# Ten plain-form steps for the sums, one PSUM exchange, and products placed by row work in a two-layer hybrid decoder

## The chip, the cores and the metric

The kernel runs on one core of a Trainium2 chip. The metric is the time of one execution in device microseconds (us). Most executions agree within 0.3%.

The engines named here are TensorE (PE, with its weight loads as PEld), VectorE (DVE), ScalarE (ACT), GpSimd (POOL) and SyncE (SP), whose queue issues most DMAs. SBUF is the memory that the engines compute from; PSUM holds what PE writes, in banks that are handed out as named buffers.

## The reference

One inference step of a two-layer decoder on a prompt of 1024 tokens and on 8 sequences of 4 new tokens (32 rows), width 1024. Each layer projects x, mixes along time in three groups of heads, projects back, and runs a gated ConvFFN of width 2816. Both residuals are scaled by ALPHA and normed.

```python
p_rw, p_gl, p_rt = split(x @ w_in[l])
y_a, sh, s_a = _rwkv7_mix(p_rw, ...)     # scan over time, state (H,64,64)
y_b, s_b = _gla_mix(p_gl, ...)           # chunks of 64
y_c, s_c = _ret_mix(p_rt, ...)           # chunks of 64
mix = concatenate([y_a, y_b, y_c], -1) @ w_out[l]
x = _layer_norm(ALPHA * x + mix, ...)
u = x @ w_up                             # 1024 -> 2 * 2816
c = conv_b + sum(conv_w[j] * buf[:, j:j + t_] for j in range(3))
a, b = split(c, 2)
f = (gelu(a) * b) @ w_down               # 2816 -> 1024
x = _layer_norm(ALPHA * x + f, ...)
```

Outputs are y of all tokens and the new states of every mixer and of the convolution.

## The kernel before

**Tiles and precision.** Channels lie on the 128 partitions and tokens along the free dimension, in three blocks n = 0, 1, 2 of 384, 384 and 288 columns (`NB`); block 2 holds the 32 sample tokens and the last 256 prompt tokens. Every large product is made of three matmuls (`mm3`, L140 in the trace): operands are split into a high and a low part (`split`, L197: ACT makes the high part, POOL or DVE the low one), and high x high, low x high and high x low are summed in PSUM. Small products of the mixers use plain 32-bit operands.

**Order of the tensor engine.** `Tensor` keeps its own clock `t`, to which each matmul adds its columns times passes over 2400 (`order`), and chains every PE instruction to the one before it, so PE's order is the order of emission. The mixers are written as generators (`Stream`), which yield either a delay from the table `AFTER` or an event. `run` goes round: of all streams that are ready on that clock it steps the first in the list. The streams of the recurrent chains stand first and those of the large projections last (`filler`), so a projection's product (three matmuls of a `gemm` step) is emitted when no chain step is ready. DVE, ACT and POOL are ordered by the framework's own scheduler, by program order and a simulated timeline.

**Stages of a layer.** First the projection for the first token block (`group_a(0)`, tile `pa`). Then the RWKV mixer: streams `chains`, `grams`, `toks`, `fronts` (tiles `gps`, `xps`, `tps`, `ups`, `zy`, `sp`, `up`), with `groups()` as filler (the rest of `pa`, then `group_b`, tile `gt`). Then GLA and retention (tiles `gsp`, `gop`, `gup`, `rsp`, `rop`, `ytp`), with the rest of `gt` and the output projection (`out_projs`, tile `po`) at the end of the list. Then the ConvFFN.

**ConvFFN.** There are 22 pairs of up tiles, j = 0 to 21 (tile j and tile j + 22). The plain form (`up_plain`, tile `pu`) multiplies each of the two tiles by all three blocks: eight half products of 12 matmuls for the two prompt blocks, four for the sample block. The other form (`up`) takes the two tiles and two prompt blocks as a 2 x 2 block product with seven products in place of eight (tiles `pa`, `pg`, `pb`, `pc`, `pf`, `pd`, `pe`), and the sample block as before (tile `p`). It needs sums of the weights, formed on DVE for each tile, and sums of x1 (`qs`), formed once by the generator `sums()`. That generator is stepped from `then(j, i, n)` at the places named in `times`, with i the half of the pair and n the block. Before the change, j = 0 to 3 are plain and `sums()` has five steps: four for k = 0 to 3 of its first loop, and one for its whole second loop, which writes over the first four tiles of x1's block 1. Its temporaries come from the ring of six buffers "u" that the up projections use too.

The down products of the pair j - 2, j - 1 (tile `pd`, `downs`) are emitted in the middle of tile j (`between`). Each of 24 has six matmuls and is read by DVE into `acc`; in the first group (L1664) the read also adds the residual x1, high and low part in two instructions, later (L1660) it is one add.

**PSUM.** Two pools matter: "g" (`pg`) with three buffers and "d" (`pd`) with five. Each tag hands out its buffers in turn, and a product waits until the one that held its buffer before has been read. `bank(n, name)` takes "g" for block 2 and "d" for the others. In `up`, the second product (`pg`, read at L1596) is in "g" and the third (`pb`, read at L1610) in "d"; the down products after it are in "d".

Of the kernel before, what the change touches and what calls it, by code (L numbers as in the profile page):

```python
# [18 lines left out]
P = 128  # L19
# [17 lines left out]
FB, BB = 2, 3  # L37
GB = 2
# [64 lines left out]
class Tensor:  # L103


    def __init__(self, tc, engine):
        self.tc, self.engine, self.t, self.last, self.posts, self.held = tc, engine, 0.0, None, [], None
        Event.clock = self.clock
# [4 lines left out]
    def order(self, ins, cols, passes):  # L113
        if self.held is not None:
            self.held.append((ins, cols, passes))
            return
        ins = ins.ins
        if self.last is not None:
            self.tc.add_manual_dep(ins, self.last.name, mybir.DependencyInfo(mybir.DependencyClass.NoSync, mybir.DependencyReason.DATA),
                                   reason="order of the tensor engine")  # L120
        self.last = ins
        self.t += max(0.025, cols * passes / 2400)

# [14 lines left out]
    def matmul(self, out, lhsT, rhs, start, stop):  # L138
        cols = int(np.prod(rhs.shape[1:]))
        self.order(self.engine.matmul(out, lhsT, rhs, start=start, stop=stop), cols, 4 if rhs.dtype == F32 else 1)  # L140

    def transpose(self, out, in_, identity):
        self.order(self.engine.transpose(out, in_, identity), identity.shape[1], 4)
# [10 lines left out]
    def run(self, streams, filler):  # L154

        streams = list(streams)
        while streams:
            self.flush(self.t)
            ready = [s for s in streams + filler if s.at() is not None and s.ready <= self.t + 0.02]
            if not ready:  # L160
                t = [s.ready for s in streams + filler if s.at() is not None] + [p[0] for p in self.posts]
                self.t = max(self.t, min(t)) + 0.001
                continue
            s = ready[0]
            if not s.step(self.clock):
                (streams if s in streams else filler).remove(s)
# [3 lines left out]
def step_kernel(ctx: ExitStack, tc: tile.TileContext, xT, wA, wB, wO, wU, wD, pp, pb, lora, bg, bgk, shT, cvT, srw, sgl, srt,  # L170
# [150 lines left out]
    for l in range(depth):  # L321
# [1052 lines left out]
        run([Stream(g) for g in (loads(0), loads(1), gla_backs(), fronts(0), ret_backs(), fronts(1), yrows(), ln1_steps())] + filler + [Stream(out_projs())], [])  # L1374
# [98 lines left out]
        def sums():  # L1473
# [30 lines left out]
            for k in range(4):  # L1504
                d = apart(G, x(1, k + 4), x(1, k))
                two(t3[0][:, k], t3[1][:, k], d, G)
                d = apart(V, x(1, k), x(0, k))
                minus(V, x(1, k + 4), d)
                two(t2[0][:, k], t2[1][:, k], d, G)
                f = new()  # L1510
                V.tensor_tensor(f, x(0, k + 4)[0], d, ALU.subtract)
                V.tensor_tensor(f, f, x(0, k + 4)[1], ALU.add)
                two(t4[0][:, k], t4[1][:, k], f, V)
                yield
# [3 lines left out]
            yield  # L1518
# [54 lines left out]
        def up(j, qs, late=False, between=lambda: None):  # L1573
# [18 lines left out]
            p2 = pg.tile([P, 512], F32, tag="g", name="pg")[:, :384]  # L1592
# [13 lines left out]
            pb_ = bank(0, "pb")  # L1606
# [47 lines left out]
        def down(m, n, group, hs, ws):  # L1654
# [4 lines left out]
            if group:  # L1659
                V.tensor_tensor(a, a, ps, ALU.add)  # L1660
            else:

                for x, y in zip(x1[n][:2], (ps, a)):
                    V.scalar_tensor_tensor(a, x[:, m].bitcast(F32), ALPHA, y, ALU.mult, ALU.add)  # L1664
# [11 lines left out]
        times = ((1, 0, 2), (1, 1, 2), (2, 0, 2), (2, 1, 2), (3, 1, 1))  # L1676
# [5 lines left out]
        for j in range(0, NJ - 2, 2):  # L1682
# [6 lines left out]
            elif j < 4:  # L1689
# [3 lines left out]
            hs = [a, up(j + 1, qs) if j >= 4 else up_plain(j + 1, lambda: None, then)]  # L1693
# [216 lines left out]
```

## Time and profile before

| | us |
|---|---|
| median of 3 runs | 3405.08 |
| lowest, highest | 3397.25, 3408.31 |
| profiled execution | 3395.68 |
| its span, first to last instruction | 3393.9 |

Mean granted PE clock of that execution: 0.945 of full speed. The sum to be made is against the profiled execution; it stands 9.4 us below the median of the runs shown.

The trace names an instruction by line, engine, operation and `out<-in` with the kernel's tile names. Nearly every matmul has the line of the helper (L140), so tiles tell them apart. "Idle" or a bracket gives how long the engine had nothing, and "<-" what ended it. A stage's row gives busy times of the engines and, behind them, the granted PE clock.

### The profile page before, as it was taken

How to read it: one execution, taken by the hardware profiler on the slowest of the kernel's cores; microseconds unless marked ns; L12 is line 12 of the kernel's file. 1: busy time of each engine (PE TensorE's matmuls, PEld its weight loads, DVE VectorE, ACT ScalarE, POOL GpSimd, SP SyncE). 2: the span in 40 equal slices, each digit the busy share in tenths (PEclk: the TensorE clock that was granted, in tenths of full speed). 3: DMA queues.
4: the chain of work that ended last, by engine and by line, in shares of the span. 5: the costliest groups of instructions: out<-in, count | busy, mean ns of one | idle time of the engine just before them, and what ended most of it. 6: DMA issues, size and time to landing. Idle time of an engine off the chain costs nothing. (4 is left out here: it accounts for less than half of the span.)

```text
span 3393.9 us, 59056 instructions
## 1 busy us (share of the span) xinstructions
PE 3103.4 (91%) x21618; PEld 2868.3 (85%) x21618; DVE 2374.4 (70%) x5085; ACT 1577.6 (46%) x3635; POOL 1575.1 (46%) x1512
## 2 busy tenths in 40 slices
PE   8889999998889999999788899998998899999995
PEld 8778887777889999999687787876778899999994
DVE  3586764566797777777857667644667977777778
ACT  6754432654534334434586534325545334344346
POOL 5542222144655555545675422221346555455556
PEclk9989999988999999999898899998989899999997
DMA  7443223443301111111264432233433011111111
GB/s 242 147 130 83 70 68 121 120 131 104 90 26 44 56 43 46 47 54 54 96 193 142 115 78 68 65 118 113 129 114 90 25 44 54 41 51 47 54 53 66
DMA packets 245566, 291.14 MB, mean 86 GB/s; under 512 B 76620, under 2 KB 158316, under 8 KB 245276
## 3 DMA queue, kind: packets, MB, share of 16 engines
q1 hardware_dynamic: 225004, 274.08, 26.8%
q10 hardware_dynamic: 20272, 13.29, 1.6%
q8 instruction: 170, 2.79, 0.3%
q14 instruction: 120, 0.98, 0.1%
HBM read 228.85 MB, written 58.43 MB: 85 GB/s over the span
## 5 line engine op out<-in xcount | busy, mean ns | idle before, releaser
L1433 DVE SCALAR_TENSOR_TENSOR c<-u,ppt,c 128x32 f32<-128x32 f32 (+3 forms) x704 | 514.2, 762 | 71.3 <-ACT c L1437 65.9
L197 POOL TENSOR_TENSOR wil<-wir,wih 128x512 fp32r<-128x512 f32 (+1 forms) x264 | 368.7, 1407 | 253.9 <-ACT wih L197 228.8
L140 PE MATMUL gt<-wih,xh 128*128 128x320 f32 (+1 forms) x1008 | 347.5, 346 | 4.6 <-DVE mx L404 4.6
L140 PE MATMUL gt<-wil,xh 128*128 128x320 f32 (+1 forms) x1008 | 322.2, 321 | 5.8 <-POOL wil L197 5.8
L1660 DVE TENSOR_TENSOR acc<-acc,pd 128x384 f32<-128x384 f32 (+1 forms) x480 | 239.4, 517 | 112.7 <-PE pd L140 110.2
L140 PE MATMUL gt<-wih,xl 128*128 128x320 f32 x896 | 286.0, 319 | 0.0
L197 ACT CAST wih<-wir 128x512 fp32r<-128x512 f32 (+1 forms) x296 | 184.5, 636 | 131.4 <-PE po L140 57.5
L140 PE MATMUL pa<-xh,wih 128*128 128x384 f32 (+1 forms) x576 | 208.7, 362 | 29.3 <-ACT wih L197 12.4
L653 DVE TENSOR_TENSOR tm<-U,N 96x60 f32<-96x60 f32 (+24 forms) x558 | 175.1, 314 | 81.2 <-DMA N<-gd 66.1
L140 PEld LDWEIGHTS gt<-wih,xh 128*128 128x128 f32 (+1 forms) x1008 | 192.1, 191 | 42.4 <-issue 24.6
L140 PE MATMUL pa<-xh,wil 128*128 128x384 f32 (+1 forms) x576 | 197.5, 343 | 12.5 <-POOL wil L197 12.5
L140 PEld LDWEIGHTS gt<-wil,xh 128*128 128x128 f32 (+1 forms) x1008 | 193.6, 192 | 10.1 <-POOL wil L197 8.6
L140 PE MATMUL pa<-xl,wih 128*128 128x384 f32 (+1 forms) x576 | 195.7, 340 | 0.8 <-POOL xl L197 0.8
L140 PEld LDWEIGHTS gt<-wih,xl 128*128 128x128 f32 x896 | 177.2, 198 | 0.0
L655 DVE TENSOR_TENSOR U<-U,tm 96x60 f32<-96x60 f32 (+24 forms) x558 | 164.6, 295 | 16.3 <-DMA tokd<-ev 0.3
L197 POOL TENSOR_TENSOR hl<-c,hh 128x384 fp32r<-128x384 f32 x132 | 139.4, 1066 | 53.0 <-ACT hh L197 53.0
L140 PEld LDWEIGHTS pa<-xh,wih 128*128 128x128 f32 x576 | 117.3, 204 | 44.0 <-ACT wih L197 13.6
L140 PE MATMUL po<-yh,wih 128*128 128x384 f32 (+1 forms) x384 | 136.1, 354 | 12.1 <-DVE ac L1349 10.2
L1437 ACT ACTIVATE c<-u,ppt 128x384 f32<-128x384 f32 x144 | 101.8, 708 | 85.3 <-DVE u L1633 39.9
L140 PEld LDWEIGHTS pa<-xh,wil 128*128 128x128 f32 x576 | 117.0, 203 | 16.6 <-POOL wil L197 16.6
L140 PE MATMUL po<-yl,wih 128*128 128x384 f32 (+1 forms) x384 | 128.1, 334 | 0.0
L140 PE MATMUL po<-yh,wil 128*128 128x384 f32 (+1 forms) x384 | 128.0, 333 | 0.0
(967 smaller groups left out, 10199.1 us busy)
## 6 DMA issues: line engine op xcount, KB each, us to landing
wir<-in_wA_dram SPq DMA_DIRECT2D x144, 256.0 KB
wir<-in_wO_dram SPq DMA_DIRECT2D x96, 256.0 KB
wir<-in_wB_dram SPq DMA_DIRECT2D x56, 320.0 KB
tokd<-ev SPq DMA_DIRECT2D x112, 160.0 KB
x<-rkvd SPq DMA_DIRECT2D x16, 576.0 KB
tk<-tokd SPq DMA_DIRECT2D x16, 480.0 KB
rkvd<-mx SPq DMA_DIRECT2D x36, 192.0 KB
tk<-tokd SPq DMA_DIRECT2D x16, 400.0 KB
```

The source lines that it names most:

```text
L140: self.order(self.engine.matmul(out, lhsT, rhs, start=start, stop=stop), cols, 4 if rhs.dtype == F32 else 1)
L197: return A.copy(dst_h, src), (le or G).tensor_tensor(dst_l, src, dst_h.bitcast(F32), ALU.subtract)
L653: V.tensor_tensor(tm, U[:, 0:nr, i:i + 1].to_broadcast([4 * ns, nr, 31 - i]), N[:, i:i + 1, i + 1:32].to_broadcast([4 * ns, nr, 31 - i]), ...
L655: V.tensor_tensor(U[:, 0:nr, i + 1:32], U[:, 0:nr, i + 1:32], tm, ALU.add)
L1433: V.scalar_tensor_tensor(cv[..., o:], uu[..., tap + o:tap + w], pc(PP_CV + 4 * t + tap), cv[..., o:], ALU.mult, ALU.add)
L1437: A.activation(c, src, AF.Identity, scale=pc(PP_CV + 4 * t + 2), bias=pc(PP_CV + 4 * t + 3))
L1660: V.tensor_tensor(a, a, ps, ALU.add)
```

## The change

- `Tensor` now also keeps the row work of each PE instruction: columns times passes (at most 2) times the share of the 128 rows. `thin()` is true if the row work of the last 3.4 us on the planner's clock is under 0.52 of what full rows would do.
- In `run`, if it is thin, the first ready stream that is a filler or in `dense` is stepped ahead of the first ready stream of the list. In the RWKV stage the filler is `groups()`; in the GLA and retention stage `dense` holds what is left of it and `out_projs`.
- `sums()` has ten steps: each k of the first loop in two (the first half is POOL and ACT work alone), the second loop in two. `times` has ten places, from j = 1 to the end of j = 5.
- The plain form is used for j = 0 to 5.
- In `up`, `pg` comes from "d" and `pb` from "g".
- The residual's high part is added in the first group of down products as before; its low part for block 1 in the same group, for block 0 in the second and for block 2 in the third.

```diff
...
 FB, BB = 2, 3
+
+DENSE, SPAN = 0.52, 3.4
 GB = 2
 BK, XB = 1, 2
 WBUFS, RAW = 4, 4
...
     def __init__(self, tc, engine):
-        self.tc, self.engine, self.t, self.last, self.posts, self.held = tc, engine, 0.0, None, [], None
+        self.tc, self.engine, self.t, self.last, self.posts, self.held, self.work = tc, engine, 0.0, None, [], None, []
         Event.clock = self.clock
     def clock(self):
         return self.t
-    def order(self, ins, cols, passes):
+    def order(self, ins, cols, passes, rows):
         if self.held is not None:
-            self.held.append((ins, cols, passes))
+            self.held.append((ins, cols, passes, rows))
             return
         ins = ins.ins
         if self.last is not None:
...
                                    reason="order of the tensor engine")
         self.last = ins
         self.t += max(0.025, cols * passes / 2400)
+        self.work.append((self.t, cols * min(passes, 2) * rows / 128))
+
+    def thin(self):
+
+        while self.work and self.work[0][0] < self.t - SPAN:
+            self.work.pop(0)
+        return sum(w for _, w in self.work) < DENSE * SPAN * 2400
     def hold(self, do):
...
     def matmul(self, out, lhsT, rhs, start, stop):
         cols = int(np.prod(rhs.shape[1:]))
-        self.order(self.engine.matmul(out, lhsT, rhs, start=start, stop=stop), cols, 4 if rhs.dtype == F32 else 1)
+        self.order(self.engine.matmul(out, lhsT, rhs, start=start, stop=stop), cols, 4 if rhs.dtype == F32 else 1, lhsT.shape[0])
     def transpose(self, out, in_, identity):
-        self.order(self.engine.transpose(out, in_, identity), identity.shape[1], 4)
+        self.order(self.engine.transpose(out, in_, identity), identity.shape[1], 4, in_.shape[0])
     def post(self, after, do):
...
             self.posts.remove(p)
             p[2]()
-    def run(self, streams, filler):
+    def run(self, streams, filler, dense=()):
+
         streams = list(streams)
         while streams:
...
                 self.t = max(self.t, min(t)) + 0.001
                 continue
             s = ready[0]
+            if self.thin():
+                s = next((x for x in ready if x in filler or x in dense), s)
             if not s.step(self.clock):
                 (streams if s in streams else filler).remove(s)
...
             for n in range(2):
                 yield ln1_at[n]
                 yield from ln1[n].steps(ppt[:, PP_LN:PP_LN + 16], x1[n], feed.ends)
-        run([Stream(g) for g in (loads(0), loads(1), gla_backs(), fronts(0), ret_backs(), fronts(1), yrows(), ln1_steps())] + filler + [Stream(out_projs())], [])
+        po_ = [Stream(out_projs())]
+        run([Stream(g) for g in (loads(0), loads(1), gla_backs(), fronts(0), ret_backs(), fronts(1), yrows(), ln1_steps())] + filler + po_, [], filler + po_)
         TE.flush(1e9)
         nc.sync.dma_start(o_glp[l, 0:P], sg[:, 0])
         nc.sync.dma_start(o_glp[l, P:160], sg[:32, 1])
...
             for k in range(4):
                 d = apart(G, x(1, k + 4), x(1, k))
                 two(t3[0][:, k], t3[1][:, k], d, G)
+                yield
                 d = apart(V, x(1, k), x(0, k))
                 minus(V, x(1, k + 4), d)
                 two(t2[0][:, k], t2[1][:, k], d, G)
...
             for k in range(4):
                 d = apart(V if k % 2 else G, x(1, k), x(0, k))
                 two(h1[:, k], l1[:, k], d, V)
-            yield
+                if k % 2:
+                    yield
         def product(ps, w, x, first=True, last=True):
...
             if not late:
                 product(p0, w, x2[1], False, True)
                 c20, u20 = conv_samples(t0, 0, p0)
-            p2 = pg.tile([P, 512], F32, tag="g", name="pg")[:, :384]
+            p2 = bank(0, "pg")
             product(p2, w, b21)
             u11 = new_u()
             v11, v22 = u11[:, 2:386], u22[:, 2:386]
...
             V.tensor_tensor(r21, r11, r21, ALU.subtract)
             V.tensor_tensor(r11, s1, r11, ALU.subtract)
             V.tensor_tensor(r12, r12, r11, ALU.subtract)
-            pb_ = bank(0, "pb")
+            pb_ = pg.tile([P, 512], F32, tag="g", name="pb")[:, :384]
             product(pb_, piece(r11, "s2"), q2)
             u12 = new_u()
             v12 = u12[:, 2:386]
...
             a = acc[n][m]
             if group:
                 V.tensor_tensor(a, a, ps, ALU.add)
-            else:
-
-                for x, y in zip(x1[n][:2], (ps, a)):
-                    V.scalar_tensor_tensor(a, x[:, m].bitcast(F32), ALPHA, y, ALU.mult, ALU.add)
+
+            for i, x in enumerate(x1[n][:2]):
+                if group == (i and (1, 0, 2)[n]):
+                    V.scalar_tensor_tensor(a, x[:, m].bitcast(F32), ALPHA, a if group or i else ps, ALU.mult, ALU.add)
         def downs(j, hs, group):
             for half in range(2):
...
         make = sums()
         qs = next(make)
-        times = ((1, 0, 2), (1, 1, 2), (2, 0, 2), (2, 1, 2), (3, 1, 1))
+        times = ((1, 0, 1), (1, 1, 1), (2, 0, 0), (2, 1, 2), (3, 0, 1), (3, 1, 1), (4, 0, 0), (4, 1, 2), (5, 1, 1), (5, 1, 2))
         def then(*at):
             if at in times:
...
                     downs(j - 2, hs, j // 2 - 1)
             if j == 0:
                 a = up_first()
-            elif j < 4:
+            elif j < 6:
                 a = up_plain(j, between, then)
             else:
                 a = up(j, qs, between=between)
-            hs = [a, up(j + 1, qs) if j >= 4 else up_plain(j + 1, lambda: None, then)]
+            hs = [a, up(j + 1, qs) if j >= 6 else up_plain(j + 1, lambda: None, then)]
         xs = [None] * 3
```

## What it will do to the time

> **What bounds the kernel now.** I read the head of the page, the chain that ended last, the busy time by stage, the waits of the tensor engine (PE), and then single stretches.
>
> ```profile
> span 3393.9 us, 59056 instructions
> DVE 2%; PE 1%; ACT 1%; issue 0%; POOL 0%; DMA 0%; DVEq 0%; ACTq 0%; POOLq 0%
> 140.00:560.00 420.00, 390.77 (x3430) 343.53 (x3431) 287.90 (x1037) 178.16 (x408) 131.77 (x142) 0.93 0.33 91
> 560.00:881.00 321.00, 289.55 (x2168) 240.63 (x2166) 203.33 (x360) 168.00 (x392) 116.59 (x97) 0.91 0.41 126
> 881.00:1660.00 779.00, 744.20 (x4540) 733.76 (x4541) 605.58 (x990) 327.75 (x790) 437.18 (x411) 0.98 0.16 47
> 1810.00:2260.00 450.00, 411.91 (x3524) 361.55 (x3523) 303.56 (x1052) 182.10 (x416) 143.54 (x151) 0.92 0.32 89
> 2260.00:2580.00 320.00, 276.72 (x2117) 230.00 (x2115) 193.95 (x347) 168.34 (x392) 110.77 (x93) 0.91 0.40 124
> 2580.00:3394.00 814.00, 749.66 (x4552) 737.79 (x4552) 627.78 (x1030) 351.34 (x827) 456.66 (x422) 0.96 0.16 49
> ```
>
> The chain reaches back over only some 5% of the span, so it can't price a change in the middle. The other rows are stages: length, busy time (and count) of PE, weight loads, DVE, ACT, POOL, then the granted PE clock, DMA share and GB/s. Both layers have the same three: RWKV mixer (140 to 560, 1810 to 2260), GLA and retention with the output projection (to 881 and 2580), and ConvFFN (to 1660 and 3394). In each, PE is busy over 86% of the time and DVE, ACT and POOL nowhere over 78%. So PE's own order decides: a time is gained where PE waits less, has fewer products, or runs less at a reduced clock. What PE waited for, over the whole span:
>
> ```profile
> PE pd L140 <- DVE u L1610: 15.3, 16, 2.0
> PE pd L140 <- ACT c L1437: 11.9, 4, 4.6
> PE p L140 <- ACT c L1437: 10.7, 2, 5.4
> PE pd L140 <- DVE acc L1664: 8.3, 2, 4.2
> ```
>
> (total, times, longest, in us). All four are in the ConvFFN, where the diff's other edits lie. Where they sit, and the steady state to hold them against:
>
> ```profile
> 945.00:985.00 40.00, 30.34 (x164) 28.09 (x163) 38.74 (x67) 11.34 (x28) 19.18 (x18) 0.83 0.12 40
> 1010.00:1060.00 50.00, 44.63 (x268) 44.31 (x267) 37.74 (x58) 17.84 (x44) 26.83 (x25) 0.93 0.15 43
> 2642.00:2682.00 40.00, 29.38 (x152) 27.54 (x151) 38.71 (x64) 11.29 (x28) 20.51 (x19) 0.79 0.13 40
> 2707.00:2757.00 50.00, 44.62 (x262) 44.30 (x261) 37.77 (x58) 17.84 (x44) 26.86 (x25) 0.93 0.15 43
> 1109.00:1175.00 66.00, 65.56 (x408) 64.98 (x408) 49.23 (x84) 26.80 (x67) 35.37 (x35) 1.00 0.16 49
> ```
>
> In the steady pair of tiles a matmul takes 65.56/408 = 0.161 us. At that rate the four stretches hold 26.4, 43.1, 24.5 and 42.2 us of work, so they lose 13.6, 6.9, 15.5 and 7.8: 43.8 us. Of this 11.9 + 10.7 + 8.3 = 30.9 is waiting. The other 13 is the clock (0.83, 0.93, 0.79, 0.93), which drops behind a long wait. In the first and third DVE is 97% busy: there PE waits for DVE.
>
> **The sums in ten steps.** The sums of x1 that the seven-product form needs are DVE, ACT and POOL work; no DMA goes with them. Their groups in the first ConvFFN, and the residual adds beside them:
>
> ```profile
> L1664 DVE SCALAR_TENSOR_TENSOR acc<-x1l,acc 128x384 f32<-128x384 f32 (+1 forms) x24 | 16.5, 696 | 0.0
> L1664 DVE SCALAR_TENSOR_TENSOR acc<-x1h,pd 128x384 f32<-128x384 f32 (+1 forms) x24 | 12.0, 505 | 0.0
> L1503 DVE TENSOR_TENSOR d<-d,x1l 128x384 f32<-128x384 f32 x4 | 5.4, 1357 | 0.1
> L1495 DVE TENSOR_TENSOR d<-x1h,x1h 128x384 f32<-128x384 f32 x6 | 4.7, 790 | 0.1
> L1512 DVE TENSOR_TENSOR d<-d,x1l 128x384 f32<-128x384 f32 x4 | 4.4, 1088 | 0.0
> L1497 DVE TENSOR_TENSOR d<-d 128x384 f32<-128x384 f32 x6 | 4.1, 689 | 0.1
> L1511 DVE TENSOR_TENSOR d<-x1h,d 128x384 f32<-128x384 f32 x4 | 3.0, 751 | 0.0
> ```
>
> The five shown are 24 instructions in 21.6 us, 0.9 each; the code issues 42 a layer on DVE, so some 38 us (42 x 0.9). Now three of the four first-loop steps (8 DVE instructions each) are issued ahead of the first down products, and those products then need 48 residual adds (28.5 us) to free their buffers. After the change one whole step and the POOL half of a second come ahead of them: 16 instructions, 14 us, less in front. The adds there fall from 48 to 32, 16 x 0.59 = 9 us less; the rest go to two later groups. The waits in that place sum to 11.9 + 8.3 = 20.2 for both layers, 10 a layer: 14 us less DVE work ahead covers them. I leave 2 us a layer: 13.6 + 15.5 - 4 = **25 us gained**.
>
> The wait of 5.4 us in each second stretch comes from the second loop of the sums (10 DVE and 6 POOL instructions at once at j = 3). It moves to the end of j = 5, in two halves, and only the first half stands ahead of the last up projection's taps. Half the cause: I take half of 6.9 + 7.8, **7 us gained**; the ends are 0 and 14.7.
>
> What is late next is DVE, over the whole stretch of the first six tiles:
>
> ```profile
> 883.30:1109.00 225.70, 208.19 (x1229) 203.30 (x1229) 180.97 (x278) 96.97 (x241) 133.88 (x126) 0.94 0.16 42
> ```
>
> It is busy 181 of 226 us, 80% (75% in the steady pair). The plain form at j = 4 and 5 has none of the seven-product form's 22 extra DVE adds (some 0.6 each, 13 us), so 168 us of DVE work stand in some 208 us: 81%, enough if it is spread evenly. Where it isn't, the 25 us are lost piece by piece (second rival).
>
> **Two more tiles in plain form.** Each of j = 4 and 5 has eight prompt products for seven. One product, from the chain that ended last:
>
> ```profile
> 3292.30 2.08 PE pc L140 x12
> ```
>
> Four of them (two tiles, two layers): 4 x 2.08 = **8.3 us lost**, in full, since PE is the bound. Weight pieces and their DMAs are the same eight a tile; ACT and POOL split four in place of seven.
>
> **pb in the other PSUM pool.** The first down products of a pair take the five buffers "d" in turn, and the fifth stands behind pb, which DVE reads late (L1610):
>
> ```profile
> 1105.80 0.54 DVE L1596 TENSOR_TENSOR u<-u,pg 128x384 f32<-128x384 f32 x1
> ...
> 1108.36 0.55 DVE L1610 TENSOR_TENSOR u<-u,pb 128x384 f32<-128x384 f32 x1
> 1108.83 1.47 DVE L1660 TENSOR_TENSOR acc<-acc,pd 128x384 f32<-128x384 f32 x3
> 1108.97 0.45 PE L140 MATMUL pd<-hh,wD4wh 128*128 128x384 f32 x1 [0.87 <-DVE u L1610]
> ```
>
> With pg in that ring, read by 1106.34, the fifth can start at once, at 1108.97 - 0.87 = 1108.10. It takes 1.04 us (six matmuls, half of 2.08), to 1109.14. The sixth then stands behind the first read of L1660, which ends near 1109.37 in the same DVE order. So 0.25 of 0.87 us remains: 15.3 x 0.7 = **10 us gained** of at most 15.3. In the pool "g" pb takes the buffer of the pb of the tile before, read long since; I cost that at nothing, and if the two p's beside it were late, pb would wait for them as p now does (up to 5.4 us once a layer).
>
> Sum for the ConvFFN: 25 + 7 + 10 - 8.3 = **34 us gained**, from 8 lost (nothing freed) to 51 gained (43.8 + 15.3 - 8.3).
>
> **Products ahead of chain steps in the mixers.** The clock there is 0.91 to 0.93. Below full it is 0.50, so the time at half clock is twice the missing share: 59 + 58 + 72 + 58 = 247 us, 72 windows of 3.41 us. What sends it there:
>
> ```profile
> L197 POOL TENSOR_TENSOR wil<-wir,wih 128x512 fp32r<-128x512 f32 (+1 forms) x264 | 368.7, 1407 | 253.9 <-ACT wih L197 228.8
> ...
> 94.50:97.91 3.41, 1.97 (x10) 1.66 (x11) 0.81 (x2) 3.38 (x7) 1.71 (x2) 1.00 0.15 43
> 97.91:101.33 3.42, 2.28 (x13) 1.96 (x12) 2.03 (x4) 3.42 (x10) 3.42 (x4) 1.00 0.40 132
> 657.67:661.09 3.42, 2.87 (x36) 2.19 (x32) 2.49 (x6) 2.28 (x13) 0.00 (x0) 1.00 0.73 239
> 661.09:664.50 3.41, 3.41 (x22) 2.95 (x19) 1.94 (x5) 1.47 (x3) 0.49 (x1) 0.50 0.35 100
> L140 PE MATMUL gop<-tk,at 64*64 64x64 f32 x12 | 0.5, 218 | 0.0
> 560.00:720.00 160.00, 60.44 (x323) 50.35 (x321) 4.80 (x10) 6.45 (x15) 0.90 0.43 133
> 2260.00:2412.00 152.00, 53.97 (x273) 44.05 (x271) 4.33 (x9) 5.19 (x12) 0.91 0.40 123
> ```
>
> (The first row is of the page's groups, the others are of stretches.) Ten products of the first projection, all on 128 rows, in 94.50:97.91, PE busy 58%, and the clock stays at 1.00. At 657.67 PE is busy 84% with 36 small matmuls, many on 64 rows or fewer (one group is shown), and the next window is at 0.50. So it is row work that counts, which is what the new rule measures. The last two rows count tile gt alone: 323 and 273 of its matmuls are issued beside those bursts, so there is something to put ahead.
>
> An averted half window saves at most 1.7 us, all 72 at most 123. But most fall behind waits, where the planner's clock sees no burst. The retention and GLA stages have 34 of the windows and nearly pure bursts of small matmuls; I take a quarter averted there (8.5 x 1.7 = 14 us), none in the RWKV stages, and 4 us back for chain steps that come later: **10 us gained**. The ends are 60 gained (half of all) and 64 lost (the last rival). A product moved ahead brings its weight's SP load and its ACT and POOL splits forward; with POOL at 31 to 36% and DMA at 32 to 41% in those stages, I cost that at nothing. Without the cover a late POOL split delays PE by up to its 1.4 us (first row).
>
> [...]
>
> Sum: 34 + 10 = 44 us off the profiled run of 3395.7 us (span 3393.9), that is 3352. The median of the runs is 3405.1, 9.4 above it, so **3361 us**.
>
> **Rivals.**
> 1. Bursts are not what drops the clock, only idle time is. Then the mixers give nothing, and the delayed chain costs the 4 us: 34 - 4 = 30 off, 3375. Against it stands 657.67; for it, that most low windows hold a wait.
> 2. The DVE backlog moves to j = 4 to 6: DVE at 80% and the sums still 38 us. Then the 32 us become 10, the mixers 0: 10 + 10 - 8.3 = 12 off, 3393.
> 3. The rule spreads the products so well that half of the 34 windows go and as many in the RWKV stages: 60 off there in clock and waits at the upper end, 30 in the middle: 64 off, 3341.
> 4. Slower: the rule takes products away too early. Nine RWKV batches with some four bursts, two steps of 0.43 us each (three 320-column matmuls of 2.08/12 x 320/384 = 0.144): 31 us a layer go ahead of the chain. The GLA stage has only 323 x 0.144 = 47 us of them. It decides from the point where gt ends before the output projection's first y is ready; then PE idles for what is missing, up to 31 a layer, 62 in all: 62 - 34 = 28 slower, 3433. Against it: the same work is due anyway, and the stage's loads wait for these very products.
>
> **How the numbers follow.** Forecast 0.45 (3345 to 3375), first rival 0.15, second 0.14, third 0.16, fourth 0.10. A difference under 0.3% (10 us: 3395 to 3415) can't be told from no change here. Faster: 0.45 + 0.15 + 0.16 and 0.06 of the second, 0.82; same 0.08, the rest of the second; slower 0.10. The range runs from the third rival's better half to the end of the second, 3325 to 3397; about 0.17 is left out, most of it above.
>
> **What would show it.** The waits at L1664 and on ACT c in those four stretches gone or under 2 us; those on u L1610 replaced by short ones on acc L1660; 48 more matmuls; the clock of 560 to 881 and 2260 to 2580 at 0.93 or more with gt ending earlier. Wrong would be: PE waits of over 3 us at j = 4 to 6, a mixer clock unchanged, or a mixer stage that is longer.

## The result, and the profile after

| | before | after |
|---|---|---|
| median, us | 3401.16 | 3363.99 |
| lowest to highest | 3391.03 to 3408.31 | 3362.72 to 3366.12 |
| runs | 4 | 4 |
| profiled execution, us | 3395.68 | 3366.12 |

The ratio is 0.9907, with a 95% interval of 0.9884 to 0.9929: 24 to 39 us less. Profiled execution against profiled execution it is 29.6 us less.

In the changed kernel every matmul of the helper has line L149 (L140 before), the residual's adds stand at L1679 (L1664), the plain adds into `acc` at L1675 (L1660), `split` at L209 and the read of `pb` at L1625.

The head of the page, and the waits of PE in the first ConvFFN (total us, times, longest):

```profile
span 3364.1 us, 59024 instructions
PE 3105.8 (92%) x21666; PEld 2870.5 (85%) x21666; DVE 2347.1 (70%) x5041; ACT 1568.2 (47%) x3627; POOL 1556.3 (46%) x1496
```

```profile
PE pd L149 <- DVE acc L1675: 7.8, 10, 3.4
...
PE pd L149 <- DVE acc L1679: 2.0, 2, 1.1
PE pd L149 <- ACT wD5wh L209: 1.0, 1, 1.0
PE pd L149 <- POOL wD5wl L209: 1.0, 1, 1.0
```

There are 48 more matmuls than the 21618 before, as many as four products of 12. None of the four large waits of before is left: those on `u` and on ACT's `c` ahead of `p` are gone, `pd` waits 0.5 us for `c`, and the wait on the residual is down to two of about 1 us. There are more waits on the plain adds, 10 in this layer for 2 before; the longest, 3.4 us, stands at the last down products, where 3.9 us stood before. New are the waits on the pieces of one weight, `wD5`.

The four stretches that the prediction priced, at their new places (length, busy time and count of PE, PEld, DVE, ACT, POOL, then PE clock, DMA share, GB/s; so in all rows of stretches below):

```profile
958.00:998.00 40.00, 37.52 (x214) 36.37 (x213) 29.07 (x52) 9.90 (x25) 14.99 (x14) 0.91 0.14 46
1010.00:1060.00 50.00, 47.81 (x299) 47.42 (x298) 39.12 (x64) 18.52 (x47) 26.69 (x26) 1.00 0.14 43
2624.00:2664.00 40.00, 36.74 (x217) 35.77 (x216) 29.36 (x53) 9.90 (x25) 15.34 (x14) 0.96 0.15 47
2690.00:2740.00 50.00, 47.83 (x299) 47.44 (x298) 38.82 (x64) 16.75 (x44) 24.16 (x23) 1.00 0.13 38
```

DVE, at 97% before in the first and third, is now busy 73% there. At 0.161 us a matmul the stretches lose 5.5, 1.9, 5.1 and 1.9 us, in place of 13.6, 6.9, 15.5 and 7.8.

To see the whole, I cut each ConvFFN at its first down product, the first with `wD2`, the first with `wD6` and the last. Before, then after, three rows for each layer:

```profile
947.67:1038.24 90.57, 75.53 (x434) 72.97 (x433) 83.18 (x125) 32.84 (x86) 53.44 (x49) 0.89 0.08 26
1038.24:1169.96 131.72, 130.85 (x818) 130.32 (x817) 97.62 (x168) 53.60 (x131) 68.19 (x67) 1.00 0.16 49
1169.96:1660.92 490.96, 475.93 (x2932) 470.38 (x2932) 378.50 (x632) 205.65 (x488) 272.82 (x258) 0.99 0.16 49
2644.25:2737.13 92.88, 76.89 (x435) 74.72 (x433) 85.42 (x129) 32.09 (x83) 54.06 (x50) 0.87 0.08 26
2737.13:2868.79 131.66, 130.79 (x817) 130.15 (x817) 96.80 (x166) 53.64 (x131) 68.02 (x64) 1.00 0.16 49
2868.79:3358.37 489.58, 475.45 (x2932) 470.18 (x2932) 377.04 (x631) 205.23 (x488) 272.23 (x258) 0.99 0.15 48
```

```profile
960.62:1035.81 75.19, 72.71 (x435) 71.56 (x434) 57.07 (x88) 28.21 (x74) 40.26 (x39) 0.95 0.13 43
1035.81:1176.23 140.42, 136.27 (x842) 135.24 (x841) 113.08 (x183) 54.19 (x136) 72.52 (x68) 0.99 0.12 37
1176.23:1663.19 486.96, 477.40 (x2932) 471.59 (x2932) 376.38 (x631) 205.63 (x488) 273.15 (x258) 0.99 0.16 49
2627.04:2701.78 74.74, 71.48 (x434) 70.51 (x433) 56.95 (x88) 28.18 (x74) 40.22 (x39) 0.98 0.14 43
2701.78:2842.85 141.07, 136.48 (x842) 135.20 (x841) 114.38 (x183) 54.23 (x137) 71.63 (x68) 0.99 0.12 36
2842.85:3329.24 486.39, 477.46 (x2932) 472.01 (x2932) 376.49 (x632) 206.14 (x489) 273.08 (x258) 0.99 0.15 48
```

The first part gains 15.4 and 18.1 us. The second, which ran without loss before (818 x 0.161 = 131.7), is 8.7 and 9.4 longer; its 24 more matmuls are 3.9 of that. The third gains 4.0 and 3.2. Together 22.6 us.

The mixers, from the first `gps` to the first `gop` (RWKV) and from there to the ConvFFN (GLA, retention, output projection), for both layers; before, then after:

```profile
106.37:596.02 489.65, 450.43 (x3801) 394.50 (x3800) 324.17 (x1112) 206.53 (x479) 166.35 (x177) 0.93 0.35 102
596.02:883.26 287.24, 259.45 (x1984) 216.76 (x1982) 189.25 (x335) 160.85 (x367) 102.24 (x84) 0.91 0.40 120
1780.15:2278.80 498.65, 453.06 (x3794) 398.33 (x3793) 328.29 (x1114) 205.12 (x477) 166.06 (x176) 0.92 0.35 99
2278.80:2579.99 301.19, 261.92 (x2009) 217.12 (x2007) 187.75 (x335) 162.82 (x370) 104.81 (x87) 0.91 0.39 118
```

```profile
105.71:595.08 489.37, 449.58 (x3807) 393.58 (x3807) 320.14 (x1112) 206.65 (x479) 167.88 (x176) 0.94 0.36 102
595.08:895.79 300.71, 266.12 (x1977) 221.81 (x1975) 186.28 (x337) 158.43 (x364) 101.76 (x84) 0.87 0.38 115
1782.19:2269.38 487.19, 443.15 (x3798) 388.65 (x3797) 332.17 (x1113) 204.17 (x478) 163.70 (x174) 0.95 0.35 101
2269.38:2562.79 293.41, 261.05 (x2005) 216.81 (x2002) 195.57 (x337) 161.36 (x369) 109.61 (x88) 0.92 0.40 121
```

The first layer's GLA stage is 13.5 us longer, at a clock of 0.87 for 0.91; the second layer's stages are 11.5 and 7.8 shorter. The four sum to 6.0 less. With the ConvFFN's 22.6 that is 28.6 of the 29.6 us.

### The profile page after: what moved, and what is told of

Same layout as the page of the kernel before. It is cut to its first block, busy times and chain, and to the rows that moved or that the text cites. A ratio compares the mean times of both kernels' runs of the same rounds, so it can differ in the third digit from the quotient of the medians.

```text
span 3364.1 us, 59024 instructions
## 1 busy us (share of the span) xinstructions
PE 3105.8 (92%) x21666; PEld 2870.5 (85%) x21666; DVE 2347.1 (70%) x5041; ACT 1568.2 (47%) x3627; POOL 1556.3 (46%) x1496
## 5 line engine op out<-in xcount | busy, mean ns | idle before, releaser
L209 POOL TENSOR_TENSOR wil<-wir,wih 128x512 fp32r<-128x512 f32 (+1 forms) x264 | 370.1, 1412 | 277.6 <-ACT wih L209 231.4
L149 PE MATMUL gt<-wih,xh 128*128 128x320 f32 (+1 forms) x1008 | 345.6, 344 | 1.4 <-DVE mx L416 1.4
L149 PE MATMUL gt<-wil,xh 128*128 128x320 f32 (+1 forms) x1008 | 319.9, 319 | 7.7 <-POOL wil L209 7.6
L1675 DVE TENSOR_TENSOR acc<-acc,pd 128x384 f32<-128x384 f32 (+1 forms) x480 | 236.5, 516 | 87.9 <-PE pd L149 86.0
L149 PE MATMUL gt<-wih,xl 128*128 128x320 f32 x896 | 284.5, 317 | 0.0
L209 ACT CAST wih<-wir 128x512 fp32r<-128x512 f32 (+1 forms) x296 | 184.9, 636 | 133.9 <-PE po L149 60.9
L149 PE MATMUL pa<-xh,wih 128*128 128x384 f32 (+1 forms) x576 | 206.6, 359 | 28.7 <-ACT wih L209 11.5
L149 PEld LDWEIGHTS gt<-wih,xh 128*128 128x128 f32 (+1 forms) x1008 | 190.2, 189 | 42.1 <-issue 25.0
L149 PE MATMUL pa<-xh,wil 128*128 128x384 f32 (+1 forms) x576 | 195.2, 339 | 12.3 <-POOL wil L209 12.1
L149 PEld LDWEIGHTS gt<-wil,xh 128*128 128x128 f32 (+1 forms) x1008 | 191.6, 190 | 13.6 <-POOL wil L209 12.2
L149 PE MATMUL pa<-xl,wih 128*128 128x384 f32 (+1 forms) x576 | 194.0, 337 | 1.2 <-POOL xl L209 1.2
L209 POOL TENSOR_TENSOR hl<-c,hh 128x384 fp32r<-128x384 f32 x132 | 139.0, 1063 | 89.7 <-ACT hh L209 89.3
L149 PEld LDWEIGHTS gt<-wih,xl 128*128 128x128 f32 x896 | 175.7, 196 | 0.0
L149 PEld LDWEIGHTS pa<-xh,wih 128*128 128x128 f32 x576 | 115.1, 200 | 44.3 <-ACT wih L209 13.3
L149 PE MATMUL po<-yh,wih 128*128 128x384 f32 (+1 forms) x384 | 137.4, 358 | 11.9 <-DVE ac L1361 8.9
L149 PE MATMUL po<-yh,wil 128*128 128x384 f32 (+1 forms) x384 | 129.6, 337 | 2.1 <-DVE wil L209 1.1
L149 PEld LDWEIGHTS pa<-xh,wil 128*128 128x128 f32 x576 | 115.2, 200 | 17.3 <-POOL wil L209 17.0
L149 PE MATMUL po<-yl,wih 128*128 128x384 f32 (+1 forms) x384 | 128.9, 336 | 0.0
L1450 ACT ACTIVATE c<-u,ppt 128x384 f32<-128x384 f32 x128 | 90.4, 708 | 75.5 <-DVE u L1648 35.4
```

The lines of the kernel that those rows point to most:

```text
L209: return A.copy(dst_h, src), (le or G).tensor_tensor(dst_l, src, dst_h.bitcast(F32), ALU.subtract)
L1450: A.activation(c, src, AF.Identity, scale=pc(PP_CV + 4 * t + 2), bias=pc(PP_CV + 4 * t + 3))
```

## The experiments

Diffs are against the kernel after, unless said otherwise. The kernel before ran beside each group; ratios are to it.

**Each half alone.** The ConvFFN edits without the placing, run in two groups:

```diff
-            if self.thin():
-                s = next((x for x in ready if x in filler or x in dense), s)
```

> The changed kernel with the two lines in run() that step a filler first taken out: the ConvFFN's edits alone. Before 3401, after 3364 (37 less). Theory: the ConvFFN's edits give some 22 to 30 and the placing of products the rest, so 3371 to 3379, slower than the changed kernel by 7 to 15. Rival A: the placing gives nothing, the two layers' mixers (12 longer, 20 shorter in one profile) are chance: 3364. Rival B: it costs time by the longer GLA stage of the first layer: under 3358.

> The kernel without the placing once more, beside the others of this call. Theory: 3364 to 3374 and within 0.3% of the changed kernel's ratio of 0.9907, so that the placing in both layers is worth nothing; the stage of the first layer's GLA 286 to 288 again.

Measured: 3369.06 us, ratio 0.9896 (0.9864 to 0.9928), and 3373.59, 0.9931 (0.9915 to 0.9948). The placing alone, with the ConvFFN as before; against the kernel before, with `thin()` and its bookkeeping:

```diff
+            if self.thin():
+                s = next((x for x in ready if x in filler or x in dense), s)
```

> The kernel before with the placing of products alone (row work, thin(), run() and the dense list), ConvFFN as before. Theory: 3386 to 3394 (7 to 15 less). Rival A: 3401 as before. Rival B: 3405 or more. If the parts add up, its gain and that of the ConvFFN alone make 37 together.

Measured: 3400.57, 0.9993 (0.9974 to 1.0011). Both first expectations gave the placing 7 to 15 us; their rivals A, which gave it nothing, came. The ConvFFN edits carry the gain; the placing in both layers gives nothing that can be measured.

**How far a mixer stage varies by itself.** The kernel before, once more with a profile:

> The kernel before once more, for its stages. Theory: its ConvFFN parts come back within 1 us (65, 91 to 93, 132, 490 per layer: start to first down product, to the second group, to the fourth, to the last), while the RWKV and GLA stages move by up to 10 us without any change of the program. Rival: the mixers repeat within 2 us too, so that the 6 to 10 us by which the RWKV stages of the kernel with the ConvFFN alone were shorter belong to the change.

Measured: 3392.40, 0.9983 (0.9957 to 1.0008). Its stages beside those of the first profile: RWKV 483.6 (489.7) and 492.6 (498.7), GLA 286.7 (287.2) and 312.8 (301.2). The two profiles of the ConvFFN edits alone have 480.0 and 492.7 in the first RWKV stage. In both pairs PE's order in the mixers is the same, matmul for matmul. So one program's mixer stage moves by up to 13 us between profiles, and one pair of profiles proves nothing there. The profiles of all the runs together do (us, by the same borders; those with another bar are left out, and a run with the rule in one place counts in the rows that this leaves pure):

| stage | rule off: profiles, mean (range) | rule on: profiles, mean (range) | difference |
|---|---|---|---|
| RWKV, first layer | 6, 486.1 (480 to 493) | 6, 491.4 (488 to 497) | +5 |
| GLA, first layer | 5, 287.8 (283 to 296) | 6, 301.9 (298 to 304) | +14 |
| RWKV, second layer | 5, 495.0 (493 to 499) | 7, 488.1 (486 to 493) | -7 |
| GLA, second layer | 4, 305.7 (301 to 313) | 7, 293.4 (293 to 294) | -12 |

By these means the rule costs the first layer 19 us and saves the second 19. In the GLA rows the ranges don't touch; in the RWKV rows they overlap.

The two layers differ only ahead of the fifth burst of `rop` in the GLA stage. In the first layer it begins 120 us into the stage with the rule off (117 to 126) and 143 with it on (142 to 145), in the second 147 (143 to 153) and 143 (140 to 144). From there to the end of the stage the rule saves both: 168 becomes 159 us, and 159 becomes 151.

**Where the placing acts.** In the GLA run alone:

```diff
-                s = next((x for x in ready if x in filler or x in dense), s)
+                s = next((x for x in ready if x in dense), s)
```

> The changed kernel with the placing in the GLA and retention run alone; in the RWKV run the list's first ready stream goes. The PE order of the RWKV stages differs between before and after by at most 12 matmuls. Theory: nothing to lose there, so 3361 to 3368. Rival: the RWKV stage of the second layer, 5 to 8 us shorter in the profile, owes that to the placing: 3369 to 3373.

Measured: 3389.58, 0.9959 (0.9937 to 0.9980), slower than with the rule in both runs (3363.99) and than without it. Its GLA stages:

```profile
586.10:878.20 292.10, 262.72 (x1984) 219.39 (x1982) 191.92 (x335) 156.49 (x363) 101.56 (x83) 0.90 0.39 118
2259.70:2579.30 319.60, 276.02 (x2013) 227.19 (x2006) 193.21 (x338) 165.27 (x372) 110.39 (x88) 0.86 0.36 112
```

Both expectations missed: the second layer's stage is the longest of all. PE's order in the RWKV stages is here that of the kernels without the rule. So at this bar (0.52) the second layer's GLA stage gained only with the rule in the RWKV stage before it. The rule in the RWKV stage alone wasn't tried.

In the second layer alone, which the table speaks for:

```diff
+        TE.placing = l > 0
...
-            if self.thin():
+            if self.placing and self.thin():
```

> The changed kernel with the placing in the second layer alone. By stages of the runs so far the placing makes the first layer's RWKV and GLA stages 8 and 15 us longer and the second layer's 8 and 13 shorter. Theory: the stages add, so this is 17 to 25 us under the changed kernel, 3339 to 3348 (ratio to before 0.982 to 0.986). Rival: the second layer's gain hangs on how the first left the planner's clock, as the run with the placing in the GLA stages alone suggests (second layer 319.6 there): 3355 to 3375.

Measured: 3351.17, 0.9872 (0.9852 to 0.9893), the fastest of all, but short of the 3339 to 3348 that were expected. It is 22 us below the ConvFFN edits alone of the same group (0.9931; the intervals are apart) and 12.8 below the kernel after, which ran in another group (the intervals just overlap). PE's order in its second layer's mixers is that of the kernel after, matmul for matmul, and in its first that of the kernel before: what the rule does in one layer doesn't reach PE's order in the other. Its profiled execution was the slowest of its five (3364.12). Its second GLA stage is like the others with the rule, its first the longest of those without:

```profile
594.00:889.63 295.63, 268.67 (x1984) 224.23 (x1981) 189.59 (x335) 161.33 (x367) 102.26 (x84) 0.88 0.37 117
...
2265.63:2559.56 293.93, 260.80 (x2005) 217.36 (x2003) 195.16 (x338) 161.37 (x369) 109.48 (x88) 0.92 0.39 121
```

**When the placing acts.** A lower and a higher bar:

```diff
-DENSE, SPAN = 0.52, 3.4
+DENSE, SPAN = 0.35, 3.4
```

> The changed kernel with the threshold of the rule at 0.35 in place of 0.52: fewer products go ahead. Theory (each product put ahead delays a chain step, what it saves in clock is chance): the first layer's GLA stage comes back part of the way, 288 to 297, the second layer's lies between 293 and 306. Rival (row work is what counts): more half windows in both layers and both GLA stages longer than the changed kernel's 301 and 293.

> The changed kernel with the threshold at 0.70: more products go ahead, also beside bursts that real row work covers. Theory: longer GLA stages, 305 to 320 in the first layer, 295 to 310 in the second, with the mean clock of those stages no higher than 0.92. Rival: a clock of 0.95 or more in them and both stages shorter than 293.

Measured: 0.35 gives 3369.47, 0.9907 (0.9886 to 0.9927), with GLA stages of 287.4 and 296.8 us; 0.70 gives 3371.61, 0.9929 (0.9911 to 0.9947). The stages of the second:

```profile
104.83:605.62 500.79, 457.77 (x3882) 400.03 (x3881) 327.49 (x1115) 206.35 (x483) 167.51 (x177) 0.95 0.34 101
605.62:901.20 295.58, 257.39 (x1903) 213.09 (x1900) 185.59 (x332) 153.49 (x359) 99.56 (x84) 0.86 0.36 113
```

At 0.35 the first layer's GLA stage is as without the rule and the second's keeps most of its gain, near the lengths expected. Both RWKV stages (494.0 and 496.2) have no gain, and PE's order in them is that of the kernels without the rule. The four stages sum to 1574.3, about the 1576.7 of before. So at this bar, in one profile, the second GLA stage gains without the rule acting in the RWKV stage before it. At 0.70 the lengths missed: longer GLA stages were expected, 305 to 320 and 295 to 310, and they are 295.6 and 287.8, shorter than at 0.52 (300.7 and 293.4). Some 75 matmuls have moved from the first layer's GLA stage (1977 to 1903) into its RWKV stage (3807 to 3882), which is the longest of all. Filler work is a fixed amount, and what fills one burst is missing at a later one: the four sum to 1574.7.

**The sums and the plain tiles.** Two more plain tiles with the first loop in its four steps at the old places and the second loop whole at j = 5:

```diff
-                yield
...
-                if k % 2:
-                    yield
+            yield
...
-        times = ((1, 0, 1), (1, 1, 1), (2, 0, 0), (2, 1, 2), (3, 0, 1), (3, 1, 1), (4, 0, 0), (4, 1, 2), (5, 1, 1), (5, 1, 2))
+        times = ((1, 0, 2), (1, 1, 2), (2, 0, 2), (2, 1, 2), (5, 1, 1))
```

> The changed kernel with the first loop of the sums in four whole steps at the places of before (j = 1 and 2), and its second loop in one step at the end of j = 5; six plain tiles, the PSUM exchange and the spread residual stay. Theory: three first-loop steps stand ahead of the first down products again, so DVE is late: the part of 75 becomes 81 to 86 per layer, in all 10 to 22 us longer than 3364, and a wait on DVE or ACT c of 3 to 7 us returns there. Rival: the residual's spread and the plain tiles alone were enough: 75 to 77.

Measured: 3374.04, 0.9948 (0.9932 to 0.9965), with the first parts and the wait on `c` as expected. Its first two parts in the first layer, and PE's wait on `c` over the whole span:

```profile
958.22:1041.39 83.17, 73.17 (x435) 71.83 (x433) 63.74 (x98) 32.81 (x86) 42.67 (x42) 0.92 0.14 44
1041.39:1176.38 134.99, 134.27 (x842) 133.95 (x841) 106.15 (x174) 51.80 (x130) 66.97 (x64) 1.00 0.12 38
```

```profile
PE pd L149 <- ACT c L1450: 12.2, 4, 4.5
```

Ten steps squeezed into j = 1 to 3, with four plain tiles:

```diff
-        times = ((1, 0, 1), (1, 1, 1), (2, 0, 0), (2, 1, 2), (3, 0, 1), (3, 1, 1), (4, 0, 0), (4, 1, 2), (5, 1, 1), (5, 1, 2))
+        times = ((1, 0, 1), (1, 1, 1), (2, 0, 0), (2, 1, 0), (2, 1, 2), (3, 0, 0), (3, 0, 1), (3, 0, 2), (3, 1, 1), (3, 1, 2))
...
-            elif j < 6:
+            elif j < 4:
...
-            hs = [a, up(j + 1, qs) if j >= 6 else up_plain(j + 1, lambda: None, then)]
+            hs = [a, up(j + 1, qs) if j >= 4 else up_plain(j + 1, lambda: None, then)]
```

> The changed kernel with four plain tiles as before: the ten steps keep their places up to (2, 0, 0) and the other seven follow in j = 2 and 3. It has 48 matmuls fewer (8.3 us). Theory: DVE has some 56 us of work in the 61 us of those tiles, so PE waits once or twice for it: 2 to 6 us lost per layer of the 4.2 saved, in all 3356 to 3370. Rival A: DVE keeps up, 3354 to 3357. Rival B: the second loop's wait of 5.4 us on ACT c comes back with the clock's drop behind it: 3370 to 3376.

Measured: 3375.47, 0.9943 (0.9921 to 0.9965), as its rival B had it. First parts 86.3 and 87.2 us, second parts 134.7 and 135.4; its largest wait:

```profile
PE pb L149 <- ACT c L1450: 20.6, 2, 10.9
```

Of the first part's 33.5 us (both layers) the plain tiles with the second loop moved to j = 5 bring 15.2 and the steps without the plain tiles 9.9, 25.1 together. The first of these runs has the waits of the first loop as before (12.2 us on `c`, 8.3 on the residual) and is rid of the second loop's, ahead of `p`. The other is rid of the first loop's, and the second loop's comes back larger, at `pb`. So the steps need the plain tiles' room. The second part shows a price: with the second loop whole and no finer steps, 842 matmuls take 134.99 us, their bare 842 x 0.161 = 135.6; with the finer steps 140.42. Over both parts the finer steps are worth only 2.6 and 4.1 us in the two layers.

**The residual's adds**, all in the first group again:

```diff
-                if group == (i and (1, 0, 2)[n]):
+                if group == 0:
```

> The changed kernel with both parts of the residual added in the first group of down products again, 48 reads and adds in place of 32. Theory: DVE has 9 us more to do there per layer, of which the slack that the moved sums leave covers about half: the part from the first to the second group is 75 now and becomes 77 to 81, in all 4 to 10 us longer than 3364. Rival: the sums' place alone decides: within 2 us of 75 and of 3364.

Measured: 3369.74, 0.9928 (0.9908 to 0.9949); first parts 75.1 and 75.3 us, as after. The 77 to 81 us that were expected did not come: spreading the adds brings nothing that shows.

**The PSUM exchange undone:**

```diff
-            p2 = bank(0, "pg")
+            p2 = pg.tile([P, 512], F32, tag="g", name="pg")[:, :384]
...
-            pb_ = pg.tile([P, 512], F32, tag="g", name="pb")[:, :384]
+            pb_ = bank(0, "pb")
```

> The changed kernel with pg back in the pool g and pb back in d. Theory: the down products wait for pb again, some 0.9 us in each of 14 to 16 pairs, 8 to 10 in all, so 3372 to 3374 and a row of PE waits on DVE u (pb) of 12 to 15 us. Rival: DVE is late there in any case and the wait only changes its name: within 3 us of 3364.

Measured: 3375.49, 0.9920 (0.9891 to 0.9949), 11.5 us above the kernel after, as expected, but with intervals that overlap (by the ratios it is 4 us). The profiles show it better: the wait on `u` is back, and the third parts take 492.4 and 496.0 us. Over all profiles they average 487.5 and 487.0 us with the exchange (10 profiles) and 493.8 and 492.2 without (4), 11.4 us in sum.

```profile
PE pd L149 <- DVE u L1625: 16.9, 14, 2.0
```

## Why the prediction came out as it did

**The total.** 3361 was forecast, 3364 measured, inside the range. The terms did less well: 44 us off the profiled execution were to give 3352, and it is 3366, 14.4 more. The kernel before had been profiled 9.4 us under the median taken and that of after 2.1 over its own; these 11.5 us hide all but 2.9 of the miss. That the total came so close is luck.

**Sums and first down products: right in sum.** 25 + 7 = 32 us were forecast, 33.5 came in the first parts. By the four stretches the split is 18.5 and 10.9: "half the cause" was too little for the second loop's wait, which went whole. The argument of 14 us less DVE work ahead was enough alone; the 9 us of residual adds were not needed. That the steps would bring so little without the two plain tiles (9.9) it didn't see.

**Two more plain tiles: right.** 24 more matmuls a layer, 3.9 us each, 7.8 for 8.3.

**"81%, enough if it is spread evenly": the first step that failed.** It was costed at nothing. DVE is at 81% in the second part (113.08 of 140.42), and that part loses 4.9 and 5.5 us, 10.4 in all: about half of the 22 us that the second rival took off. PE's waits there (the bracket is idle time and what ended it), and the stretches ahead of the first and of the other two:

```profile
1044.51 0.44 PE L149 MATMUL pd<-hh,wD2wh 128*128 128x384 f32 x1 [2.19 <-DVE acc L1675]
...
1108.80 0.44 PE L149 MATMUL pd<-hh,wD5wh 128*128 128x384 f32 x1 [1.00 <-ACT wD5wh L209]
...
1110.38 0.44 PE L149 MATMUL pd<-hh,wD5wl 128*128 128x384 f32 x1 [0.97 <-POOL wD5wl L209]
```

```profile
1017.69:1032.95 15.26, 15.26 (x96) 15.26 (x95) 14.51 (x23) 6.62 (x17) 9.01 (x10) 1.00 0.24 69
1092.00:1108.00 16.00, 15.80 (x106) 15.48 (x104) 15.66 (x19) 5.97 (x17) 12.68 (x11) 1.00 0.10 34
```

The share of the whole part hides that DVE is busy 95% and 98% of the time just ahead of the waits, where the steps of the sums stand. The run with plain tiles and no finer steps has no step at the first place; from the same `c` instructions on, DVE is busy there 9.52 of 12.75 us:

```profile
1023.88:1036.63 12.75, 12.75 (x81) 12.75 (x80) 9.52 (x15) 5.53 (x15) 6.51 (x9) 1.00 0.21 62
```

What follows in order comes late. DVE, then ACT, in the kernel after:

```profile
1038.59 1.91 DVE L1446 SCALAR_TENSOR_TENSOR c<-u,ppt,c 128x384 f32<-128x384 f32 x2 [1.59 <-ACT c L1450]
1040.42 0.54 DVE L1675 TENSOR_TENSOR acc<-acc,pd 128x384 f32<-128x384 f32 x1
1042.45 0.92 DVE L1446 SCALAR_TENSOR_TENSOR c<-u,ppt,c 128x32 f32<-128x32 f32 x2 [1.49 <-ACT c L1450]
```

```profile
1103.37 0.52 ACT L1502 CAST x1h<-d 128x384 fp32r<-128x384 f32 x1 [5.14 <-DVE d L1510]
1107.80 0.43 ACT L209 CAST hh<-c 128x288 fp32r<-128x288 f32 x1 [1.77 <-DVE c L1480]
1108.14 0.61 ACT L209 CAST wD5wh<-wD5r 128x512 fp32r<-128x512 f32 x1
```

At 1038 to 1042 DVE idles for ACT with an add into `acc` behind the wait. The run without finer steps has the same idle times there (1.59 and 1.49) and PE doesn't wait: its first `wD2` product stands 1.9 us ahead of DVE's first read of one, here 4.6. At 1098 to 1103 ACT idles 5.14 us at a cast of the sums that waits for DVE, and the split of `wD5`, in order behind it, comes 1.0 us late. The other run has the whole second loop there, with DVE as busy, and PE waits 0.7 us where it waits 2.0 here. So it is not DVE's work alone: PE comes earlier against it, and part of the lead that PE won in the first part is spent on that work in the second.

DVE is also slower there. In the kernel after, L1480 (128x384), whose operands are all in SBUF, takes 0.55 us in the median where POOL is idle (38 cases) and 1.53 where POOL is at work for over 80% of the instruction's time (46 cases); L1675, which reads PSUM, takes 0.55 in both. The steps bring POOL work as well, 12.68 of the 16.00 us in the second stretch.

**The exchange: right.** 10 us forecast; the third parts gained 7.2 by the first pair of profiles, 11.2 against the second profile of before and 11.4 over all profiles. The small waits on `acc` that were to be left are there.

**ConvFFN in sum:** 34 forecast, 22.6 by the first pair of profiles, 27 against the second profile of before, and 24 over all profiles (1427 to 1435 us without the edits in three, 1403 to 1411 with all of them in seven). The 10.4 us that the second part loses are what is missing.

**"A quarter averted ... 4 us back": the second step that failed.** 10 us were to be gained in the mixers, and the gain is nothing: 0.9993 for the placing alone, and +5, +14, -7 and -12 by stage. "None in the RWKV stages" was wrong both ways by the means, though their ranges overlap. In the first layer's GLA stage the windows at half clock went from 16 (before) to 22, in the second's from 16 and 26 (two profiles of before) to 15. The fifth `rop` burst of the first layer begins 142 us into the stage, 118 with the rule off (kernel after and its ConvFFN edits alone), yet only 24 more matmuls, 3.9 us at 0.161, stand ahead of it. The rest is what follows from the new order: 14 windows at half clock ahead of that burst for 5 (at most 1.7 us each, half of 3.41), and 15.6 us in which PE waits for 8.4. One such place; PE's timeline of the kernel after, and the stretch from its second line on:

```profile
736.93 0.52 PE L149 MATMUL po<-yh,wil 128*128 128x384 f32 x1
737.38 0.90 PE L149 MATMUL rop<-tk,qk 128*64 128x64 f32 x10
738.22 2.40 PE L149 MATMUL rop<-tk,rat 128*128 128x64 f32 x10
740.41 1.78 PE L149 MATMUL rop<-sr,rqT 128*128 128x128 f32 x6
742.12 0.66 PE L149 MATMUL gup<-tk 64*32 64x64 f32 x20
```

```profile
737.38:744.25 6.87, 6.31 (x63) 5.61 (x64) 1.98 (x5) 1.46 (x6) 0.33 (x1) 0.50 0.06 18
```

From 737.38 on no product comes for 8.67 us, until 746.05; the row has 6.87 of them, at a clock of 0.50. Two chain steps stand there, `rop` and then `gup` with the first of `gop`. The rule looks back over 3.4 us between steps; `rop` alone takes 4.7 us, and it can't fill a step that is longer. Why no product came between the two is not shown.

**"It is row work that counts, which is what the new rule measures": the third step that failed.** By the kernel's code the rule counts a plain 32-bit matmul with two passes, while its clock runs on for four. So a burst of such matmuls that fills the 3.4 us reads 0.50 at most, even on all 128 rows, and is always thin at a bar of 0.52. By the count of the last section such a burst is nearly full work: `zy<-sav,gm` on 128 rows has a record of 64 columns every 0.058 us, at two passes 0.92. The rule therefore also puts products ahead of bursts that by this count need none (above 0.45 no fall followed in 808 windows before). What that alone costs no run shows.

**The rivals.** The first had the mixers' outcome, nothing, but not for its cause: the clock fell behind low row work (behind 45 of the 45 windows under 0.35 of full work before, last section). The second came in part. The third is out. The fourth is out as a whole: the chain comes later in the first layer, as it had it, but the second layer gives that back. Of the signs that were to speak against the forecast, "a mixer stage that is longer" showed. The waits at j = 4 to 6 stayed at 2.2 us and less, under the 3 us that were named.

**What stays open:** why the same rule costs the first layer 23 us ahead of the fifth `rop` burst and the second none. With it, both GLA stages run alike (the burst 142 and 143 us in); with the ConvFFN edits alone they are at 118 and 146, and PE waits 8.4 us ahead of it in the first and 22.5 in the second. Open too is how the RWKV stage bears on the GLA stage behind it: with the rule off in it the second layer lost its gain at a bar of 0.52, and at 0.35, where the rule changes nothing in it, most of the gain was there.

## What to carry to other kernels

Work in the way of a critical buffer is worth spreading together with room to spread it into (33.5 us in the first parts here, 15.2 and 9.9 for either alone), and its price is then read in the stage that receives it: by how busy the engine is just ahead of each wait (DVE 95% and 98% here) and what stands behind that in order, not by its share of the whole stage (81%). Filler products that are put ahead are taken from a later burst (some 75 matmuls at the bar of 0.70), so such a rule is judged stage by stage and over several executions, and kept where it pays (here one layer, 0.9872 for 0.9907, with intervals that just overlap). Where a forecast goes from a profile to a median, the offset between them is a term with an error of its own, here as large as the smaller terms.

## What the hardware showed beside this

**The clock went by row work.** In the clock record of both traces the granted clock is 1.00 or 0.50, and its stretches, up to the last, are whole multiples of 3.41 us: of the 51 at half clock before, 23 are one such window long, of the 45 after, 19. I cut both traces into these windows and counted for each window at full clock the columns of its matmuls, times the passes, times the share of 128 rows, over the planner's 2400 a microsecond. A record of split operands has one pass (384 columns every 0.173 us); a plain 32-bit matmul stands as two records of two passes each (64 columns of `zy<-sav,gm` every 0.058 us). Before, with under 0.35 of full work the next window was at half clock in 45 of 45 cases, between 0.35 and 0.45 in 6 of 26, above that in none of 808. After, it was 40 of 41, 5 of 27 and none of 810; over the traces of all runs 589 of 594, 88 of 350 and 7 of 11357. In these counts the best single bar lies near 0.36: it misjudges 4 of the 879 windows before; the best bar on PE's busy share misjudges 15, and the best on the rule's own weight (one pass a plain record) 17. The windows ahead of a fall were not idle: in the kernel after, PE was busy 6% to 74% of the time in all 45 of them.

**Equal programs differ in the mixers.** The kernel before had the second layer's GLA stage at 301.2 and 312.8 us, with PE's order the same matmul for matmul. The windows at half clock go with it: 16 in the one, 26 in the other. What causes it no run shows.
